# The inverse of a DeltaNet's 32x32 blocks, from 16x16 blocks and a merge on TensorE

## The chip, the cores and the metric

The kernel runs on one core of one Trainium2 chip. The metric is the device time of one execution in microseconds. The core has five engines that work side by side: PE (TensorE, matmuls; PEld is its weight load), DVE (VectorE), ACT (ScalarE), POOL (GpSimd) and SP, which issues DMAs. Each serves its own queue in order and waits on semaphores for the others.

## What is computed

One layer of a hybrid network over 640 tokens (128 context, 512 latent) with 1024 channels: a combined input projection, a bidirectional gated DeltaNet beside a short gated convolution, a gated merge, and a SwiGLU feed-forward network. The part that matters here is the DeltaNet's chunk step. For each direction, head and chunk of 64 tokens it inverts a unit lower triangular 64x64 matrix:

```python
kb = k * beta[..., None]
lower = jnp.where(tri_strict, jnp.einsum('bhncd,bhned->bhnce', kb, k) * decay, 0.0)
eye = jnp.eye(CHUNK, dtype=jnp.float32)
tmat = lax.linalg.triangular_solve(eye + lower, jnp.broadcast_to(eye, lower.shape),
                                   left_side=True, lower=True)
u = jnp.einsum('bhnce,bhned->bhncd', tmat, v * beta[..., None])
```

There are 2 directions x 8 heads x 10 chunks = 160 such matrices, and the inverse `tmat` feeds the sequential scan over the chunks.

## The kernel before

All large products are done as three single-pass matmuls of split operands (`mm3`, lines 83 to 85): the weights arrive by DMA, ACT casts a high part `wh` (line 57) and DVE subtracts to get a low part `wl` (line 58). One projection tile of 128 channels is 2 x 8 x 3 = 48 matmuls of 320 columns that write the PSUM tile `d`. These projections are independent of the DeltaNet's chain, and PE runs them between the DeltaNet's small matmuls.

The DeltaNet is done for two heads at a time, in four pairs. `run` calls `prep(p)` and `scan(p)` for each pair with projections (`zgate`, `gate_th`, `short`) between. The calls carry priorities (1000 for `prepare`, 300000 for `scan`), and a list scheduler sorts all instructions of the program into one fixed order per engine by priority, readiness and its own idea of durations. On the chip each engine then keeps to its order, and waits where an operand is late.

`prepare` goes through these steps for one pair. It transposes q, k, v to token layout, normalises them (`ss`, `rn` and the short chain of lines 71 to 77), makes `kh`, `kt` and `bv`, transposes `kh` and `qh` on PE (line 479) and forms the decay matrices `em` and `ea`. Line 528 forms the products and lines 532 to 534 multiply them in. Then comes the inverse:

- `Md` receives the 32x32 diagonal blocks of `em`, one block per row of 32 partitions, 20 of them (2 directions x 2 heads x 5), for four quadrants of partitions (`quad`). A 32x32 block transposition on DVE (line 550) turns this into `B`, in which every partition holds one whole 32x32 block.
- Lines 551 and 552 set `X` to -B with ones on the diagonal. The loop in lines 553 to 558 is a forward substitution, all 128 partitions at once: for j = 1 to 30 a product of column j of B with row j of X (line 556, into `otmp`) and a subtraction from the rows below (line 558). These are 60 DVE instructions per pair, each needing the one before, with (31 - j) j elements per partition, 30 to 240.
- Lines 562 and 563 transpose back to `RT` (transposed inverses) and `R`, and ACT copies them into `EW` (lines 565, 566).
- The merge of two 32x32 inverses into the 64x64 inverse is done on PE: 40 matmuls of 32x32 (line 575) into PSUM tile `v`, an ACT copy `Y` (line 580), 40 more (lines 586, 587), which go in turn to four places of the array, and scaled copies into `EW` (lines 590, 592).

`scan` (line 611 on) takes `EW`: products with `kt` (line 611), then eight sequential steps of small matmuls (line 640), copies to `RS` by ACT and DVE (lines 644, 658), the output products (line 670), a normalisation on DVE (`so`, `ro`, `ob`, lines 675 to 680) and a transposition of `ob` on PE (line 684).

POOL makes `KU` (line 459), `qh`, `kl` and the triangular masks, and issues DMAs. The PSUM pools for `v`, `s` and `w` have one buffer each.

Of the kernel before, what the change touches and what calls it, by code (L numbers as in the profile page):

```python
# [9 lines left out]
F32 = mybir.dt.float32  # L10
# [3 lines left out]
ALU = mybir.AluOpType  # L14
# [4 lines left out]
P = 128  # L19
# [18 lines left out]
class Kernel:  # L38
# [369 lines left out]
    def prepare(self, p, qkv):  # L408
        nc, dn, dc, g = self.nc, self.da, self.dc, self.g
        mm = nc.tensor.matmul  # L410
# [6 lines left out]
        for j in (1, 0, 2):  # L417
            pw = self.psw.tile([P, 1024], F32, name="w", tag="w")
            for t in range(NT):
                nc.tensor.transpose(pw[:, t * P:(t + 1) * P], qkv[j][:, t * P:(t + 1) * P], self.ident)  # L420
            x = dn.tile([P, TOK], F32, name="tk", tag="t25")
            (nc.scalar.copy, nc.scalar.copy, nc.scalar.copy)[j](out=x, in_=pw[:, 0:TOK])
            tok[j] = x
        q, k, v = (tok[j] for j in range(3))
# [31 lines left out]
        for c2 in range(2):  # L456
            s = half(1 - c2)
            for d in range(2):
                nc.gpsimd.tensor_tensor(out=KU[s, d, c2], in1=bc(g["egl"][s, d, :, h2], 64),
                                        in0=self.ident[s, s].unsqueeze(1).unsqueeze(1).broadcast_to([64, NT, 2, 64]),  # L460
                                        op=ALU.mult)
# [14 lines left out]
        for j, x in enumerate((kh, qh)):  # L476
            pw = self.psw.tile([P, 1024], F32, name="w", tag="w")
# [17 lines left out]
        for c2 in range(2):  # L495
            for t_, d, i in ((em, 0, 0), (em, 1, 2), (ea, 0, 0), (ea, 1, 1)):
                nc.sync.dma_start(out=t_[c2 * 64:c2 * 64 + 64, d].rearrange("p h t x -> p (h t x)"),
                                  in_=g["scr"][i, c2, h2].rearrange("h t x -> (h t x)").unsqueeze(0).broadcast_to([64, TOK]))
# [7 lines left out]
        for c2 in range(2):  # L506
            s = slice(c2 * 64, c2 * 64 + 64)
            o = em[s].rearrange("p d h t x -> p (d h t) x")
            nc.gpsimd.affine_select(out=o, in_=o, pattern=[[0, 20], [-1, 64]], compare_op=ALU.is_gt, fill=NEG,
                                    base=0, channel_multiplier=1)  # L510
            o = fm(ea[s, 0])
            nc.gpsimd.affine_select(out=o, in_=o, pattern=[[0, 10], [1, 64]], compare_op=ALU.is_ge, fill=NEG,
                                    base=0, channel_multiplier=-1)
            o = fm(ea[s, 1])
# [7 lines left out]
        for hd in range(2):  # L522
            hs = slice(hd * 64, hd * 64 + 64)
            pw = self.psw.tile([P, 1024], F32, name="w", tag="w")
            for t in range(NT):
                for c2 in range(2):
                    n = 2 * t + c2
                    mm(pw[c2 * 64:c2 * 64 + 64, t * P:(t + 1) * P], lhsT=kq3[hs, 0, n, :], rhs=kq3[hs, :, n, :],
                       start=True, stop=True)
# [5 lines left out]
        for c2 in range(2):  # L535
            nc.gpsimd.dma_start(out=AQ[half(c2), :, c2].rearrange("p d h t x -> p d (h t x)"),
                              in_=ea[half(c2)].rearrange("p d h t x -> p d (h t x)"))


        Md, EW = self.Md, self.EW  # L540
        emv = em.rearrange("p d h t x -> p (d h t) x")
        Ev = [EW[:, :, c2].rearrange("p d h t x -> p d (h t) x") for c2 in range(2)]
        quad = [(c2, b, slice(c2 * 64 + b * 32, c2 * 64 + b * 32 + 32)) for c2 in range(2) for b in range(2)]
        for c2, b, s in quad:
            cp = (nc.vector.tensor_copy, nc.scalar.copy)[b]
            cp(out=Md[s, 0:20], in_=emv[s, :, b * 32:b * 32 + 32])
        B = dn.tile([P, 32, 32], F32, name="blk", tag="kb")
        X = dn.tile([P, 32, 32], F32, name="X")
        tmp = dn.tile([P, 256], F32, name="otmp")
        nc.vector.transpose(out=B.rearrange("q r x -> q x r"), in_=Md.rearrange("p m x -> p x m"))  # L550
        nc.vector.tensor_scalar(out=X, in0=B, scalar1=-1.0, scalar2=None, op0=ALU.mult)
        nc.vector.memset(X.rearrange("q r x -> q (r x)")[:, 0:32 * 32:33], 1.0)
        for j in range(1, 31):
            n = 31 - j
            t = tmp[:, 0:n * j].rearrange("q (a b) -> q a b", b=j)
            nc.vector.tensor_tensor(out=t, in0=B[:, j + 1:32, j:j + 1].broadcast_to([P, n, j]),  # L556
                                    in1=X[:, j:j + 1, 0:j].broadcast_to([P, n, j]), op=ALU.mult)
            nc.vector.tensor_tensor(out=X[:, j + 1:32, 0:j], in0=X[:, j + 1:32, 0:j], in1=t, op=ALU.subtract)  # L558

        RT = dn.tile([P, 32, 32], F32, name="RT", tag="kb")  # L560
        R = dn.tile([P, 32, 32], F32, name="R")
        nc.vector.transpose(out=RT.rearrange("p m x -> p x m"), in_=X)
        nc.vector.transpose(out=R.rearrange("p m x -> p x m"), in_=X.rearrange("q r x -> q x r"))
        for c2, b, s in quad:
            nc.scalar.copy(out=Ev[c2][s, 0, :, b * 32:b * 32 + 32], in_=RT[s, 0:10])
            nc.scalar.copy(out=Ev[c2][s, 1, :, b * 32:b * 32 + 32], in_=R[s, 10:20])
# [2 lines left out]
        pw = self.psv.tile([P, 1024], F32, name="v", tag="v")  # L569
        Y = dn.tile([P, 20, 32], F32, name="Y")  # L570
        for m in range(20):
            for c2 in range(2):
# [3 lines left out]
                   tile_position=(c2 * 64 + 32, c2 * 64))  # L576
# [159 lines left out]
    def run(self):  # L736
# [121 lines left out]
        dast, da = stack("da")  # L858
# [15 lines left out]
        nc.gpsimd.memset(self.EW, 0.0)  # L874
        self.Md = da.tile([P, 32, 32], F32, name="Md")
        nc.gpsimd.memset(self.Md, 0.0)
        pre = {}

        def prep(p):
# [549 lines left out]
```

## Time and profile before

| | us |
|---|---|
| median of 3 runs | 1088.66 |
| lowest, highest | 1086.5, 1089.34 |
| the profiled execution | 1085.4 |
| its span in the profile | 1083.6 |
| PE busy | 1024.1 |
| DVE busy | 835.8 |

The span runs from the first to the last instruction of the profile; the execution's own time adds 1.8 us around it. Busy times are the union of an engine's instructions. PE's matmuls overlap, so a busy PE is not a PE at its peak. DeltaNet work lies between about 85 and 460 us. [...]

### The profile page before, as it was taken

The page shows a single profiled execution, that of the slowest core. Times are in us where ns is not written, and L with a number is a line of the kernel's source. Part 1 is how long each engine was busy: PE and PEld are TensorE (multiplying, and loading weights), DVE is VectorE, ACT ScalarE, POOL GpSimd, SP SyncE. Part 2 cuts the span into 40 slices and gives each one's busy share as a digit, 9 for nine tenths or more (in the row PEclk, how much of TensorE's full clock was granted, in tenths as well). Part 3 has the DMA queues.
Part 4 walks back from the last instruction along what each step waited for, and adds up shares of the span by engine and source line. Part 5 has one row for each costly group of instructions (what it writes and reads, how often), then busy time and mean ns, then how long its engine had stood idle before and what let it go on. Part 6 is the DMA issues. An engine that isn't in the chain of part 4 may idle for free.

```text
span 1083.6 us, 19702 instructions
## 1 busy us (share of the span) xinstructions
PE 1024.1 (95%) x7729; PEld 929.0 (86%) x7729; DVE 835.8 (77%) x1698; ACT 484.4 (45%) x929; POOL 138.9 (13%) x168
## 2 busy tenths in 40 slices
PE   6999978988988989999998998999999999999997
PEld 3699978887887888899996887999999999788885
DVE  5767896997898897995995789888777775975336
ACT  5568436417524324434223466444445444623321
POOL 2215321062062150101000000000000000000000
PEclk9999989998998999999998998999999999999999
DMA  9435712264164276547953532323222222552214
GB/s 343 147 91 135 206 52 67 72 152 113 42 164 125 68 171 202 182 151 246 318 167 116 185 108 89 103 85 98 94 79 78 98 81 76 177 173 96 81 39 156
DMA packets 47399, 141.52 MB, mean 131 GB/s; under 512 B 9517, under 2 KB 10034, under 8 KB 47306
## 3 DMA queue, kind: packets, MB, share of 16 engines
q1 hardware_dynamic: 42746, 127.10, 36.1%
q0 software_dynamic: 4560, 13.15, 5.4%
q8 instruction: 61, 1.00, 0.4%
q14 instruction: 32, 0.26, 0.1%
HBM read 117.57 MB, written 12.18 MB: 120 GB/s over the span
## 4 chain that ended last, share of the span: by engine, by line
PE 69%; DVE 14%; DMA 2%; ACT 2%; issue 2%; SPq 0%; DVEq 0%; POOL 0%; ACTq 0%
PE acc L1163 21%; PE d L84 7%; PE d L85 7%; PE d L83 7%; PE acc L84 6%; PE acc L83 6%; PE acc L85 6%; PE d L1163 3%; DVE X L558 3%; PE s L640 2%; DVE otmp L556 2%; DVE wl L58 1%; PE v L611 1%; PE v L670 1%; DMA ea<-scr 1%
## 5 line engine op out<-in xcount | busy, mean ns | idle before, releaser
L83 PE MATMUL d<-hT,wh 128*128 128x320 f32 x720 | 227.8, 317 | 1.2 <-DVE cy L721 1.1
L84 PE MATMUL d<-hT,wh 128*128 128x320 f32 x720 | 228.6, 318 | 0.0
L85 PE MATMUL d<-hT,wl 128*128 128x320 f32 x720 | 227.8, 317 | 0.4 <-DVE wl L58 0.4
L57 ACT CAST wh<-wr 128x512 fp32r<-128x512 f32 x150 | 87.8, 618 | 143.2 <-PE d L84 74.4
L83 PEld LDWEIGHTS d<-hT,wh 128*128 128x128 f32 x720 | 137.3, 191 | 3.9 <-DVE cy L721 1.7
L85 PEld LDWEIGHTS d<-hT,wl 128*128 128x128 f32 x720 | 137.3, 191 | 3.2 <-issue 0.7
L84 PEld LDWEIGHTS d<-hT,wh 128*128 128x128 f32 x720 | 137.1, 191 | 2.9 <-issue 0.3
L58 DVE TENSOR_TENSOR wl<-wr,wh 128x512 fp32r<-128x512 f32 x150 | 104.2, 717 | 36.4 <-ACT wh L57 35.2
L1163 PE MATMUL acc<-mh,wl 128*128 128x320 f32 x280 | 86.9, 310 | 1.8 <-DVE wl L1098 1.8
L83 PE MATMUL acc<-wh,as 128*128 128x512 f32 x220 | 85.7, 390 | 2.1 <-ACT as L1297 2.1
L1163 PE MATMUL acc<-mh,wh 128*128 128x320 f32 x280 | 87.0, 311 | 0.3 <-ACT early L1177 0.3
L196 DVE SCALAR_TENSOR_TENSOR gacc<-wr,cv,gacc 128x1024 f32<-128x1024 f32 x64 | 80.1, 1278 | 9.1 <-DMA wr<-in_w_mod_dram 7.2
L1163 PE MATMUL acc<-ml,wh 128*128 128x320 f32 x280 | 86.7, 310 | 0.0
L84 PE MATMUL acc<-wl,as 128*128 128x512 f32 x220 | 85.6, 389 | 0.0
L85 PE MATMUL acc<-wh,as 128*128 128x512 f32 x220 | 85.5, 389 | 0.0
L1102 ACT CAST wh<-wr 128x512 fp32r<-128x512 f32 x66 | 40.6, 622 | 72.0 <-PE acc L1163 37.0
L1102 ACT CAST wh<-S 128x512 fp32r<-128x512 f32 x88 | 54.1, 619 | 36.4 <-PE d L1163 19.6
L1098 DVE TENSOR_TENSOR wl<-S,wh 128x512 fp32r<-128x512 f32 x88 | 60.0, 686 | 3.9 <-ACT wh L1102 3.0
L1098 DVE TENSOR_TENSOR wl<-wr,wh 128x512 fp32r<-128x512 f32 x66 | 45.3, 689 | 19.1 <-ACT wh L1102 18.2
L1163 PEld LDWEIGHTS acc<-mh,wl 128*128 128x128 f32 x280 | 52.8, 188 | 2.1 <-DVE wl L1098 2.0
L1163 PEld LDWEIGHTS acc<-mh,wh 128*128 128x128 f32 x280 | 52.7, 188 | 0.6 <-ACT early L1177 0.6
L1163 PEld LDWEIGHTS acc<-ml,wh 128*128 128x128 f32 x280 | 52.8, 189 | 0.0
(365 smaller groups left out, 2348.9 us busy)
## 6 DMA issues: line engine op xcount, KB each, us to landing
wr<-in_w_ffn_in_dram SPq DMA_DIRECT2D x48, 512.0 KB, 3.7
wr<-in_w_in_dram SPq DMA_DIRECT2D x45, 512.0 KB, 3.5
wr<-in_w_mod_dram SPq DMA_DIRECT2D x32, 512.0 KB, 4.0
wr<-in_w_ffn_out_dram SPq DMA_DIRECT2D x22, 512.0 KB, 3.4
mr<-in_w_mod_dram SPq DMA_DIRECT2D x16, 512.0 KB, 8.5
thd<-gt SPq DMA_DIRECT2D x16, 320.0 KB, 4.1
bth<-thd SPq DMA_DIRECT2D x16, 320.0 KB, 3.0
wr<-in_w_br_dram SPq DMA_DIRECT2D x8, 512.0 KB, 6.9
```

Of the source, the lines that this page charges most:

```text
L57: (high or nc.scalar.copy)(out=hi[:, s], in_=raw[:, s])
L58: (low or nc.vector).tensor_tensor(out=lo[:, s], in0=raw[:, s], in1=hi[:, s].bitcast(F32), op=ALU.subtract)
L83: mm(out, lhsT=ah, rhs=bh, start=start, stop=False)
L84: mm(out, lhsT=ah, rhs=bl, start=False, stop=False)
L85: mm(out, lhsT=al, rhs=bh, start=False, stop=stop)
L196: nc.vector.scalar_tensor_tensor(out=acc[v], in0=w, scalar=self.cv[:, k, v:v + 1], in1=acc[v], op0=ALU.mult, op1=ALU.add)
L556: nc.vector.tensor_tensor(out=t, in0=B[:, j + 1:32, j:j + 1].broadcast_to([P, n, j]), in1=X[:, j:j + 1, 0:j].broadcast_to([P, n, j]), op=A ...
L558: nc.vector.tensor_tensor(out=X[:, j + 1:32, 0:j], in0=X[:, j + 1:32, 0:j], in1=t, op=ALU.subtract)
L640: mm(ps[half(c2), o:o + 64], lhsT=w(d, c2, t, hd), rhs=R[:, d, c2, t, hd, :], start=True, stop=True)
L1098: tt = lambda o, a, b, op: nc.vector.tensor_tensor(out=o, in0=a, in1=b, op=op)
L1102: nc.scalar.copy(out=dst[0], in_=src)
L1163: nc.tensor.matmul(ps, lhsT=A[x][:, k], rhs=B[y][:, k], start=start and k == 0 and n == 0, stop=k == 3 and n == 2, skip_group_check=True)
```

## The change

The 32x32 block in a partition is now treated as two 16x16 diagonal blocks and one 16x16 block below the diagonal. `two` is a view of both diagonal blocks at once. The forward substitution runs on them together: 14 steps in place of 30, 28 instructions in place of 60, with 2 (15 - j) j elements each. After the transpositions, PE makes the missing block for each of the 80 blocks: a first group of 80 matmuls of 32x16 (line 571), an ACT copy into `Y16` (line 573), a second group of 160 matmuls with 16 rows of weights (lines 579, 581; half of them for `RT`, half for `R`), and two DVE subtractions into `RT` and `R` (lines 583, 585). The merge to 64x64 follows as before (now from line 598). `X` and `Y16` become tiles that live through all pairs and are cleared once by POOL.

```diff
-        B = dn.tile([P, 32, 32], F32, name="blk", tag="kb")
-        X = dn.tile([P, 32, 32], F32, name="X")
-        tmp = dn.tile([P, 256], F32, name="otmp")
-        nc.vector.transpose(out=B.rearrange("q r x -> q x r"), in_=Md.rearrange("p m x -> p x m"))
-        nc.vector.tensor_scalar(out=X, in0=B, scalar1=-1.0, scalar2=None, op0=ALU.mult)
-        nc.vector.memset(X.rearrange("q r x -> q (r x)")[:, 0:32 * 32:33], 1.0)
-        for j in range(1, 31):
-            n = 31 - j
-            t = tmp[:, 0:n * j].rearrange("q (a b) -> q a b", b=j)
-            nc.vector.tensor_tensor(out=t, in0=B[:, j + 1:32, j:j + 1].broadcast_to([P, n, j]),
-                                    in1=X[:, j:j + 1, 0:j].broadcast_to([P, n, j]), op=ALU.mult)
-            nc.vector.tensor_tensor(out=X[:, j + 1:32, 0:j], in0=X[:, j + 1:32, 0:j], in1=t, op=ALU.subtract)
+        B = dn.tile([P, 33 * 32], F32, name="blk", tag="kb")
+        tmp = dn.tile([P, 128], F32, name="otmp")
+        sq32 = lambda a: a[:, 0:1024].rearrange("q (r x) -> q r x", x=32)
+
+        two = lambda a: a.rearrange("q (u w) -> q u w", u=2)[:, :, 0:512].rearrange("q u (a b) -> q u a b", b=32)[:, :, :, 0:16]
+        Bd, Xd = two(B), two(X)
+        nc.vector.transpose(out=sq32(B).rearrange("q r x -> q x r"), in_=Md.rearrange("p m x -> p x m"))
+        nc.vector.tensor_scalar(out=Xd, in0=Bd, scalar1=-1.0, scalar2=None, op0=ALU.mult)
+        nc.vector.memset(X[:, 0:32 * 32:33], 1.0)
+        for j in range(1, 15):
+            n = 15 - j
+            t = tmp[:, 0:2 * n * j].rearrange("q (u a b) -> q u a b", u=2, b=j)
+            nc.vector.tensor_tensor(out=t, in0=Bd[:, :, j + 1:16, j:j + 1].broadcast_to([P, 2, n, j]),
+                                    in1=Xd[:, :, j:j + 1, 0:j].broadcast_to([P, 2, n, j]), op=ALU.mult)
+            nc.vector.tensor_tensor(out=Xd[:, :, j + 1:16, 0:j], in0=Xd[:, :, j + 1:16, 0:j], in1=t, op=ALU.subtract)
...
+        pw = self.psv.tile([P, 1024], F32, name="v", tag="v")
+        for m in range(20):
+            for c2, b, s in quad:
+                mm(pw[s, m * 16:m * 16 + 16], lhsT=emv[s, m, b * 32:b * 32 + 32], rhs=RT[s, m, 16:32], start=True, stop=True,
+                   tile_position=(s.start, s.start))
+        nc.scalar.copy(out=Y16[:, :, 16:32], in_=pw[:, 0:320].rearrange("p (m x) -> p m x", x=16))
+        pw = self.psv.tile([P, 1024], F32, name="v", tag="v")
+        for m in range(20):
+            for c2, b, s in quad:
+                h = slice(s.start, s.start + 16)
+                o = m * 16
+                mm(pw[s, o:o + 16], lhsT=R[h, m], rhs=Y16[h, m, 16:32], start=True, stop=True,
+                   tile_position=(s.start, s.start))
+                mm(pw[s, 512 + o:512 + o + 16], lhsT=Y16[h, m], rhs=R[h, m, 0:16], start=True, stop=True,
+                   tile_position=(s.start, s.start))
+        nc.vector.tensor_tensor(out=RT[:, 0:20, 16:32], in0=RT[:, 0:20, 16:32],
+                                in1=pw[:, 0:320].rearrange("p (m x) -> p m x", x=16), op=ALU.subtract)
+        nc.vector.tensor_tensor(out=R[:, 0:20, 0:16], in0=R[:, 0:20, 0:16],
+                                in1=pw[:, 512:832].rearrange("p (m x) -> p m x", x=16), op=ALU.subtract)
...
+        self.X = da.tile([P, 33 * 32], F32, name="X")
+        nc.gpsimd.memset(self.X, 0.0)
+        self.Y16 = da.tile([P, 20, 32], F32, name="Y16")
+        nc.gpsimd.memset(self.Y16, 0.0)
```

The change also moves what stands around the inverse, since the scheduler sorts anew. On PE before, at the second pair, the first merge group (line 575, from `RT` and `em`) follows 83 projection matmuls after the transposition of the first scan's `ob`:

```order
L83 MATMUL d<-hT_75,wh 128x320
L84 MATMUL d<-hT_76,wh 128x320
L85 MATMUL d<-hT_75,wl 128x320
L83 MATMUL d<-hT_75,wh 128x320
L575 MATMUL v<-RT,em 32x32 x40
L84 MATMUL d<-hT_76,wh 128x320
```

On PE of the change, at the same place, the transpositions of `ob` and `kh` and the first new group (line 571) stand close together, and line 579 begins the second group:

```order
L707 MATMUL v<-ident,ob 128x128 x5
L85 MATMUL d<-hT_75,wl 128x320
L83 MATMUL d<-hT_75,wh 128x320
L84 MATMUL d<-hT_76,wh 128x320
L479 MATMUL w<-ident,kh 128x128 x5
L85 MATMUL d<-hT_75,wl 128x320
L83 MATMUL d<-hT_75,wh 128x320
L571 MATMUL v<-RT,em 32x16 x80
L84 MATMUL d<-hT_76,wh 128x320
L85 MATMUL d<-hT_75,wl 128x320
L83 MATMUL d<-hT_75,wh 128x320
L84 MATMUL d<-hT_76,wh 128x320
```

Five projection matmuls now stand between `ob` and the first group, and four between the first and the second; behind the second group eight precede line 598 (the former 575). From the first scan's last output matmuls to the first group it was 144 projection matmuls before and is 53 now.

On DVE of the change, at the second scan's end, between `so` (line 698, formerly 675) and `ob` (line 703, formerly 680), the end of the third pair's substitution and both transpositions stand; these ten rows are a part of that piece:

```order
L561 TENSOR_TENSOR X<-X,otmp 128x2x2x13
L75 TENSOR_TENSOR ont<-ro 128x10
L559 TENSOR_TENSOR otmp<-blk,X 128x28
L76 TENSOR_TENSOR ont<-ont,onxh 128x10
L561 TENSOR_TENSOR X<-X,otmp 128x2x14
L77 SCALAR_TENSOR_TENSOR ro<-ont,ro 128x10
L565 STREAM_TRANSPOSE RT<-X 128x32x32
L75 TENSOR_TENSOR ont<-ro 128x10
L58 TENSOR_TENSOR wl<-wr,wh 128x512
L76 TENSOR_TENSOR ont<-ont,onxh 128x10
```

Before, ten larger instructions of the substitution and `kh` stood between `so` and `ob` there, and the transpositions came later.

## Rows read from the trace of the kernel before

**Rows 1.** Page, busy time by engine: us (share of the span) xinstructions.

```profile
PE 1024.1 (95%) x7729; PEld 929.0 (86%) x7729; DVE 835.8 (77%) x1698; ACT 484.4 (45%) x929; POOL 138.9 (13%) x168
```

**Rows 2.** Windows by stage: window, us, busy us (xinstructions) by engine, granted clock, DMA share, GB/s.

```profile
118.00:165.00 47.00, 41.07 (x268) 40.54 (x267) 44.66 (x114) 19.76 (x32) 10.92 (x10) 0.93 0.38 114
165.00:247.00 82.00, 74.28 (x872) 66.57 (x870) 70.67 (x166) 34.51 (x68) 21.59 (x25) 1.00 0.39 99
247.00:331.00 84.00, 76.05 (x856) 68.98 (x856) 72.21 (x172) 40.73 (x74) 26.06 (x30) 0.94 0.41 106
331.00:420.00 89.00, 81.49 (x1101) 73.46 (x1102) 74.17 (x156) 36.86 (x74) 25.06 (x29) 0.96 0.46 129
```

**Rows 3.** Windows, a stretch in which PE runs projections alone.

```profile
149.00:165.00 16.00, 16.00 (x111) 16.00 (x110) 15.10 (x45) 7.33 (x12) 0.00 (x0) 1.00 0.23 75
```

**Rows 4.** Chain that ended last, 85 to 450 us, shares by line.

```profile
by line: PE d L84 10.2%; PE d L85 9.6%; PE d L83 9.4%; DVE X L558 7.6%; PE s L640 6.7%; DVE otmp L556 6.3%; DVE wl L58 4.2%; issue 3.0%; PE v L611 2.9%; DMA ea<-scr 2.3%; DVE RT L562 2.2%; PE v L670 2.0%; DMA AQ<-ea 1.8%; PE w L528 1.7%; PE
```

**Rows 5.** Waits of PE, 85 to 490 us: waiter, releaser, total us, times, longest.

```profile
PE v L575 <- DVE RT L562: 9.6, 4, 4.5
PE w L479 <- DVE kh L448: 7.4, 3, 5.9
PE v L670 <- DVE RS L644: 5.3, 3, 2.6
PE v L684 <- DVE ob L680: 2.0, 1, 2.0
PE v L586 <- ACT Y L580: 1.7, 2, 0.9
...
```

**Rows 6.** Windows of the granted clock's four low stretches (first, last, sum).

```profile
141.10:147.90 6.80, 5.36 (x21) 5.39 (x22) 6.67 (x10) 0.00 (x0) 3.79 (x3) 0.50 0.18 60
...
332.30:339.10 6.80, 5.73 (x118) 5.37 (x122) 6.73 (x8) 4.99 (x10) 3.46 (x3) 0.50 0.37 98
sum 23.80, PE 20.91 PEld 20.07 DVE 20.05 ACT 10.76 POOL 12.39; mean PE 5.23 PEld 5.02 DVE 5.01 ACT 2.69 POOL 3.10
```

**Rows 7.** Windows of line 556 alone, then of line 558 alone.

```profile
85.00:450.00 365.00, 42.56 (x120) 0.97 0.46 125
...
85.00:450.00 365.00, 50.93 (x120) 0.97 0.46 125
```

**Rows 8.** Groups by form, 85 to 450 us: busy us, mean ns of one, idle before.

```profile
L556 DVE TENSOR_TENSOR otmp<-blk,X 128x30 f32<-128x30 f32 x8 | 1.4, 177 | 0.2
L556 DVE TENSOR_TENSOR otmp<-blk,X 128x108 f32<-128x108 f32 x8 | 2.2, 270 | 0.2
L558 DVE TENSOR_TENSOR X<-X,otmp 128x220 f32<-128x220 f32 x8 | 7.9, 982 | 0.1
L556 DVE TENSOR_TENSOR otmp<-blk,X 128x240 f32<-128x240 f32 x8 | 3.2, 401 | 0.0
L562 DVE STREAM_TRANSPOSE RT<-X 128x1024 f32<-128x1024 f32 x4 | 7.8, 1959 | 0.1
L563 DVE STREAM_TRANSPOSE R<-X 128x1024 f32<-128x1024 f32 x4 | 8.2, 2053 | 0.0
L592 DVE TENSOR_SCALAR EW<-v 32x320 f32<-32x320 f32 x8 | 3.9, 490 | 0.8 <-ACT EW L590 0.5
```

**Rows 9.** Timeline of PE, first merge group of the third and fourth pairs.

```profile
333.37 2.46 PE L575 MATMUL v<-RT,em 32*32 32x32 f32 x80 [4.48 <-DVE RT L562]
...
403.99 1.55 PE L575 MATMUL v<-RT,em 32*32 32x32 f32 x80 [0.99 <-DVE RT L562]
```

**Rows 10.** Timeline of PE, fourth pair, second merge group's end.

```profile
410.41 0.19 PE L586 MATMUL v<-Y,R 32*32 32x32 f32 x2
...
410.70 0.19 PE L587 MATMUL v<-R,Y 32*32 32x32 f32 x1
410.82 0.41 PE L84 MATMUL d<-hT,wh 128*128 128x320 f32 x1
411.07 0.31 PE L85 MATMUL d<-hT,wl 128*128 128x320 f32 x1
```

More of the change, by code (lines that the diff above doesn't have):

```diff
@@ L537, in prepare @@
                               in_=ea[half(c2)].rearrange("p d h t x -> p d (h t x)"))
-        Md, EW = self.Md, self.EW
+        Md, EW, X, Y16 = self.Md, self.EW, self.X, self.Y16
         emv = em.rearrange("p d h t x -> p (d h t) x")
@@ L561, in prepare @@
         R = dn.tile([P, 32, 32], F32, name="R")
-        nc.vector.transpose(out=RT.rearrange("p m x -> p x m"), in_=X)
-        nc.vector.transpose(out=R.rearrange("p m x -> p x m"), in_=X.rearrange("q r x -> q x r"))
+        nc.vector.transpose(out=RT.rearrange("p m x -> p x m"), in_=sq32(X))
+        nc.vector.transpose(out=R.rearrange("p m x -> p x m"), in_=sq32(X).rearrange("q r x -> q x r"))
+        pw = self.psv.tile([P, 1024], F32, name="v", tag="v")
[3 more added lines that the diff above has]
+                   tile_position=(s.start, s.start))
```

## The prediction

> **What bounds the kernel now.** I read the engines' busy time first: PE is busy 95% of the span and VectorE 77% [rows 1], so PE is the bound on average, and the question is what this one stage pays. The DeltaNet stage runs from 118 to 420 us, and the windows [rows 2] cut it at the moments when RT is ready. In its four windows PE is idle 47 - 41.1 + 82 - 74.3 + 84 - 76.1 + 89 - 81.5 = 29.1 us, while VectorE is busy 86 to 95%. The chain of waits says the same from the other side: lines 558 and 556, the forward substitution, hold 7.6 + 6.3% of 365 us, or 51 us [rows 4]. So in this stage VectorE is nearly as full as PE, and its X chain is what PE waits behind.
>
> Which waits: PE waited 9.6 us for RT, 7.4 for kh, 5.3 for RS, 2.0 for ob and 1.7 for Y [rows 5]. Idle time has a second price. [...] At half speed 23.8 us do the work of 11.9. So the most that PE can win back here is 29.1 + 11.9 = 41.0 us. After 420 us PE has its projections left and I take that part as it is.
>
> **The change, part by part.**
>
> *Removed from VectorE.* The 240 instructions of lines 556 and 558 took 42.56 + 50.93 = 93.5 us [rows 7]. The new chain has 28 per pair, 112 in all, with 28 to 112 elements each. From the rows for 30 elements (177 ns) and 108 (270 ns) [rows 8], which give 1.19 ns per element, the 28 sum to 6.6 us, so 26.5 us over four pairs. Two subtractions from PSUM per pair come in; the nearest row, a 320-element read from PSUM, takes 490 ns [rows 8], so 3.9 us. VectorE loses about 63 us of work, some 15 us of which is stretching, by my estimate from forms like this one: line 558 took 982 ns with 220 elements where line 556 needed 401 for 240 [rows 8]. The smaller scaling and the wider memset at the head of the chain move under 1 us. X and Y16 are cleared once on GpSimd and Y16 is filled four times by ScalarE; they are busy 13% and 45% of the span [rows 1], so that I cost both at nothing but for the wait for the copy, below.
>
> *Added to PE.* 20 x 4 small matmuls in the first group and 20 x 8 in the second are 240 per pair. The trace shows two records for each fp32 matmul (80 records for 40 matmuls, [rows 9]), so 480 records per pair and 1920 in all. With four places of the array in turn, as here, 34 records of the old merge started within 0.29 us: 8.8 ns apart [rows 10]. 1920 x 8.8 ns = 16.9 us. Going back to projections costs too: from the last small record to the second projection passed 0.37 us where one step takes 16.00/111 = 0.144 [rows 3, 10], so about 0.2 us for each of 8 new groups, 1.6 us. Sum **+18.5 us**, and nothing covers it, since PE serves its queue in order and has other work ready. Bounds: half the record price if 16 columns in place of 32 halve it, 8.4 + 1.6 = 10 us; or 19 ns as for the group that has two places only (80 in 1.55 us, [rows 9]), 37 + 1.6 = 39 us, because the second group sends two matmuls to one place in a row. I take 8.8, as its row has the same four places.
>
> [...]
>
> *Taken off PE's waits.* The X chain is some 17 us shorter per pair ((93.5 - 26.5) / 4), four times the longest wait for RT, 4.5 us [rows 5]. I count the waits for RT as gone, -9.6 us, and with them the two low-clock stretches that lay at the long ones (6.8 us each, as in [rows 6]), which is 6.8 us of work. **-16.4 us.**
>
> *New waits.* Y16 is copied by ScalarE between the two groups, and the order gives PE 4 projections meanwhile, 0.58 us; the old wait for Y reached 0.9 us with more cover [rows 5]. The subtractions, 2 x 0.49 us, stand between the second group and line 598 with 8 projections, 1.15 us, as cover. I take 0.5 us for each of the 8 places, **+4 us** (0 to 7).
>
> *What is late next.* The shorter chain lets the scheduler close up the stage: counted in the order, the projections between the first scan's last matmuls and the second pair's first group shrink from 144 to 53. So kh, RS and ob are met with less cover. For the second scan's ob the order before had ten X instructions and kh between so and ob; now it has eight small ones and both transposes, 1.96 + 2.05 us [rows 8], which is about 1 us more under as many projections (54 and 55). The stretching of VectorE does not vanish with the X chain, it falls on whatever is there. I take 2 us for ob and 3 us of the 15 us of stretching, **+5 us**. Waits for kh and RS with their low clock I leave as they are.
>
> **Sum:** 18.5 - 16.4 + 4 + 5 = +11 us. Against the profiled execution, 1085.4 us (span 1083.6), this is 1096.5. That execution lies 3.3 us under the median of the runs, 1088.66, and 1.1 under the fastest; I add half the distance: **1098 us**.
>
> **Rivals.**
>
> A. *VectorE was the bound, and PE closes up.* For it: the 51 us of the X chain on the path [rows 4]. The deciding point is whether idle time and low clock fall from 41.0 below 41.0 - 18.5 = 22.5 us. If all waits for RT, kh, ob and Y went (20.7 us, [rows 5]), with the low clock but for the one short stretch of 3.4 us after RS (10.2 us), and the 4 us of new waits came, the sum is 18.5 + 4 - 30.9 = -8.4 us: 1077 on the profiled execution, some 1079 for the median. Against it: the kh wait of 5.9 us comes early in the stage, and the order still has most of the first pair's X chain ahead of kh.
>
> B. *The small matmuls run one by one.* At the 19 ns of [rows 9] the term is 39 us and the time 1098 + 20 = 1118; slower by much. For it: two in a row per place. It decides from about 13 ns per record upward, 8 us above my price. [...]
>
> C. *Both sides cancel.* Idle and low clock fall to between 19 and 26 us: no change, near 1089.
>
> D. *The chain is not shorter.* If views of two blocks with rows of 1 to 14 elements cost as much as 490 ns each [rows 8], the 112 take 55 us and RT is late again: 18.5 + 4 us with no gain, about 1111.
>
> **How the numbers follow.** The measurement can tell 0.3%, 3.3 us, from no change: faster is under 1085.4, slower over 1091.9. My forecast (its own range 1088 to 1107) gets 0.50, of which 0.06 falls within 0.3%; A 0.22, of which 0.02; B 0.13; C 0.12, all within; D 0.03. The forecast's 0.50 has another 0.04 on the faster side, for a record price at its low bound. Faster: 0.20 of A and these 0.04, 0.24. Same: 0.06 + 0.02 + 0.12 = 0.20. Slower: 0.40 + 0.13 + 0.03 = 0.56. The range takes in the low bound of the record price and most of A, and of B the lower part: 1080 to 1115.
>
> **What would show it.** In the changed profile: lines 559 and 561 should sum to 25 to 30 us; the new groups on lines 571, 579 and 581 should start 8 to 10 ns apart and take 4 to 5 us per pair; PE's wait for RT should be under 3 us; waits for Y16 and for the subtracted RT should show with 0.3 to 0.8 us each; waits for kh, ob and RS should remain. The scans should end earlier, with more projections left behind the fourth. If PE's idle time between 118 us and the last scan, with half of the low-clock time, is under 22 us, A is right and I am wrong; if the records stand over 12 ns apart, B.

## The result, and the profile after

The changed kernel takes **1137.51 us** (median of 4 runs, 1134.43 to 1141.61) against 1088.51 for the kernel before (4 runs, 1086.5 to 1089.34): ratio 1.0455, 95% interval 1.0413 to 1.0498. The forecast was 1098, with a range up to 1115. The profiled execution took 1135.12 us, its span is 1133.3 us, 49.7 more than before, and the mean granted clock, the share of PE's full speed that the profile shows as granted, is 0.957, where it was 0.979 before.

The page of the changed kernel, busy time by engine and the queue that brings instructions (packets, MB, share), with the queue's row of the kernel before behind it:

```profile
PE 1058.7 (93%) x9649; PEld 961.8 (85%) x9649; DVE 787.4 (69%) x1578; ACT 480.3 (42%) x929; POOL 145.1 (13%) x170
...
q8 instruction: 76, 1.25, 0.5%
```

```profile
q8 instruction: 61, 1.00, 0.4%
```

VectorE lost 48.4 us of busy time and PE gained 34.6 [rows 1]. Waits of PE in the changed kernel, 85 to 600 us (waiter, releaser, total us, times, longest):

```profile
PE v L581 <- issue: 13.2, 6, 4.8
PE v L579 <- issue: 6.4, 4, 2.6
PE w L479 <- DVE kh L448: 5.8, 2, 4.5
PE v L693 <- DVE RS L667: 3.8, 2, 2.2
PE v L707 <- DVE ob L703: 2.6, 2, 2.4
...
PE v L571 <- DVE RT L565: 2.0, 1, 2.0
...
PE v L571 <- issue: 1.7, 1, 1.7
```

The wait for RT went from 9.6 to 2.0 us, as forecast [rows 5]. New at the top stand 13.2 + 6.4 + 1.7 = 21.3 us of idle time inside the new groups that end with "issue": by the profile no operand, no semaphore and no buffer was late. The timeline of PE shows them at the second pair (start us, us, line, tile, shapes, count, and the idle time before):

```profile
228.01 1.53 PE L571 MATMUL v<-RT,em 32*32 32x16 f32 x160
...
230.47 0.21 PE L581 MATMUL v<-R,Y 16*32 16x16 f32 x3
235.44 0.18 PE L581 MATMUL v<-R,Y 16*32 16x16 f32 x1 [4.76 <-issue]
...
238.90 0.18 PE L581 MATMUL v<-R,Y 16*32 16x16 f32 x1 [1.51 <-issue]
...
242.35 0.18 PE L581 MATMUL v<-R,Y 16*32 16x16 f32 x1 [1.51 <-issue]
```

The first group ran its 160 records in 1.53 us. The second stopped at 230.68, ran from 235.44 to 237.38, stopped, and so on, with 3.46 and 3.45 us from one restart to the next. In the trace the packets of the instruction queue start at 236.53, 240.00 and 243.46, the same 3.46 us apart. How many instructions one holds follows from the page: 1920 records and as many weight loads came in [rows 1], 3840 instructions, and 15 packets, so 256 per packet, 128 records.

The clock fell too. Its five long low stretches in the changed kernel (window, us, busy us by engine, granted clock, DMA share, GB/s):

```profile
145.80:166.30 20.50, 15.82 (x461) 14.66 (x450) 2.72 (x5) 7.29 (x15) 0.00 (x0) 0.50 0.22 75
214.10:220.90 6.80, 6.12 (x57) 6.01 (x58) 6.70 (x14) 1.44 (x2) 3.44 (x8) 0.50 0.54 106
234.50:251.60 17.10, 13.14 (x399) 12.54 (x399) 2.27 (x4) 6.56 (x14) 0.00 (x0) 0.50 0.21 53
319.90:333.50 13.60, 10.36 (x238) 9.82 (x239) 3.14 (x6) 6.17 (x13) 0.00 (x0) 0.50 0.09 32
412.00:429.10 17.10, 14.72 (x428) 13.81 (x427) 2.40 (x3) 5.46 (x12) 0.96 (x1) 0.50 0.48 160
```

Four of them lie on the four second groups. In the first pair the clock had fallen at 145.8, ahead of that group: PE had waited 2.04 us for RT, up to 144.6. Before the change no low stretch of the stage was longer than 6.8 us [rows 6]; this one is 20.5. With two more of 3.4 us it is 81.9 us between 85 and 520, of which PE was busy 66.6; before it was 23.8 with 20.9 busy [rows 6]. And PE's busy time in the same 435 us, before and then after:

```profile
85.00:520.00 435.00, 404.21 (x4140) 372.47 (x4139) 371.86 (x778) 192.69 (x358) 111.43 (x126) 0.97 0.48 137
```

```profile
85.00:520.00 435.00, 390.50 (x5704) 356.16 (x5704) 298.88 (x625) 175.11 (x333) 115.90 (x126) 0.91 0.41 114
```

So idle time rose from 30.8 to 44.5 us. A budget of the 49.7 us: the 1920 records at the 8.5 ns that line 571 shows at the full clock, 16.3; idle time, +13.7; busy time at the low clock, 66.6 - 20.9 = 45.7 us more, half of it lost, +22.9. Together 52.9, 3 us over; behind 520 us, which the budget leaves out, the low clock is 6 us shorter than before (14.7 us against 20.9). By this count the largest part is the clock, the next the records, then the idle time. What each would be worth without the others it doesn't show.

### The profile page after: what moved, and what is told of

It reads as the page before. It is cut to its first block, busy times and chain, and to the rows that moved or that the text cites. A ratio compares the mean times of both kernels' runs of the same rounds, so it can differ in the third digit from the quotient of the medians.

```text
span 1133.3 us, 23436 instructions
## 1 busy us (share of the span) xinstructions
PE 1058.7 (93%) x9649; PEld 961.8 (85%) x9649; DVE 787.4 (69%) x1578; ACT 480.3 (42%) x929; POOL 145.1 (13%) x170
## 3 DMA queue, kind: packets, MB, share of 16 engines
q8 instruction: 76, 1.25, 0.5%
## 4 chain that ended last, share of the span: by engine, by line
PE 68%; DVE 12%; issue 4%; DMA 2%; ACT 2%; POOL 1%; SPq 0%; DVEq 0%; POOLq 0%; ACTq 0%
PE acc L1190 20%; PE d L84 8%; PE d L83 8%; PE d L85 7%; PE acc L84 5%; PE acc L85 5%; PE acc L83 5%; PE d L1190 3%; PE s L663 2%; DVE otmp L559 1%; DVE X L561 1%; PE v L581 1%; PE v L693 1%; PE v L598 1%; PE w L528 1%
## 5 line engine op out<-in xcount | busy, mean ns | idle before, releaser
L85 PE MATMUL d<-hT,wl 128*128 128x320 f32 x720 | 233.3, 325 | 0.4 <-DVE wl L58 0.4
L84 PE MATMUL d<-hT,wh 128*128 128x320 f32 x720 | 232.2, 323 | 0.0
L83 PE MATMUL d<-hT,wh 128*128 128x320 f32 x720 | 231.7, 323 | 0.0
L85 PEld LDWEIGHTS d<-hT,wl 128*128 128x128 f32 x720 | 140.8, 196 | 4.0 <-issue 0.7
L84 PEld LDWEIGHTS d<-hT,wh 128*128 128x128 f32 x720 | 140.8, 196 | 2.3 <-issue 0.5
L83 PEld LDWEIGHTS d<-hT,wh 128*128 128x128 f32 x720 | 140.7, 196 | 1.9 <-issue 0.2
L1125 DVE TENSOR_TENSOR wl<-wr,wh 128x512 fp32r<-128x512 f32 x66 | 45.3, 689 | 19.5 <-ACT wh L1129 18.5
```

Of the source, the lines that this page charges most:

```text
L83: mm(out, lhsT=ah, rhs=bh, start=start, stop=False)
L84: mm(out, lhsT=ah, rhs=bl, start=False, stop=False)
L85: mm(out, lhsT=al, rhs=bh, start=False, stop=stop)
L1125: tt = lambda o, a, b, op: nc.vector.tensor_tensor(out=o, in0=a, in1=b, op=op)
```

## The experiments

Theory 1 says that the dense small matmuls outrun the supply of PE's instructions, and that the pauses bring the clock down. Theory 2 says that small matmuls hold the clock down by themselves. Theory 3, that matmuls in one place or buffer stop each other. "Issue" and "low" below are PE's idle time ended by nothing and the time at 0.50, both from 85 to 520 us; the changed kernel has 21.3 and 81.9.

**The two parts alone.** First the substitution without lines 568 to 586, which are both groups, the copy and the subtractions:

```diff
         nc.vector.transpose(out=R.rearrange("p m x -> p x m"), in_=sq32(X).rearrange("q r x -> q x r"))
-        pw = self.psv.tile([P, 1024], F32, name="v", tag="v")
-        for m in range(20):
...
-        nc.vector.tensor_tensor(out=R[:, 0:20, 0:16], in0=R[:, 0:20, 0:16],
-                                in1=pw[:, 512:832].rearrange("p (m x) -> p m x", x=16), op=ALU.subtract)
```

> This kernel has the two 16x16 forward substitutions on VectorE and none of the new small matmuls, subtractions or the copy to Y16; the quarter of each 32x32 inverse that the merge would fill keeps what the tile held, so its output is not the reference's. The PE stream is then the one of before. By the steps of the prediction the waits for RT go (-16.4 us) and later waits grow (+5 us): about 1077 us, against 1088.5 before. If VectorE's 63 us of work had been covered by PE's other work, 1086 to 1090. Theory 1 (the new groups outrun the supply of PE's instructions): no idle time of over 0.5 us ended by nothing (issue) on PE in the stage, and low-clock time of 30 us or less.

Measured 1083.6 us, ratio 0.9966 (0.9941 to 0.9991): 4.5 us faster than before, where 11 were expected. Its largest waits:

```profile
PE w L479 <- DVE otmp L559: 4.5, 1, 4.5
PE v L688 <- ACT sq L430: 3.9, 1, 3.9
PE v L579 <- issue: 3.6, 2, 3.0
PE w L479 <- DVE kh L448: 3.3, 2, 2.1
PE v L674 <- DVE RS L648: 2.5, 2, 2.4
PE v L579 <- DVE RT L565: 2.0, 1, 2.0
```

RT's wait fell by 7.6 us. Waits at line 479, whose operand is still `kh` behind a VectorE queue, were 7.4 and are 7.8, and `sq` and two pauses of the old merge (here line 579) came in. Idle time fell by 4.4 us only, and the low clock did not fall: 27.3 us. The chain did get shorter: the last transposition of `ob` starts at 422.0 us, where it was 462.1 before (485.7 in the changed kernel). But PE is as busy as before, 1023.6 us against 1024.1, so that 40 us less of chain were worth 4.5 us.

Then both groups and the copy to `Y16` on the old substitution, with nobody to read the results:

```diff
         nc.vector.transpose(out=R.rearrange("p m x -> p x m"), in_=X.rearrange("q r x -> q x r"))
+        pw = self.psv.tile([P, 1024], F32, name="v", tag="v")
+        for m in range(20):
+            for c2, b, s in quad:
+                mm(pw[s, m * 16:m * 16 + 16], lhsT=emv[s, m, b * 32:b * 32 + 32], rhs=RT[s, m, 16:32], start=True, stop=True,
+                   tile_position=(s.start, s.start))
...
```

> The kernel before with its 32x32 substitution, plus the 240 small matmuls per pair and the copy to Y16; nobody reads their results. This isolates what the small matmuls cost PE. At the price of the prediction (8.8 ns per record, 8 switches) it would be 1088.5 + 18.5 = 1107 us. Theory 1 (instruction supply): the second group of each pair stops after each 128 records as in the changed kernel, 4 to 8 us of such idle time per pair, and the clock falls there: 1088.5 + 18.5 + 14 to 20 of pauses + 10 to 20 of low clock = 1125 to 1145 us. If the pauses come from the shorter VectorE chain or the subtractions, no pauses and 1107 us.

Measured 1142.67 us, 1.0501 (1.0463 to 1.0538): 54.6 us over its own kernel before (1088.11). Issue 18.1, low 95.6. From the substitution alone to the changed kernel it is 53.9. The groups cost the same 54 us on either substitution, so that the cost is theirs and needs neither VectorE's shorter chain nor the subtractions.

**The order inside the second group.**

```diff
                 mm(pw[s, o:o + 16], lhsT=R[h, m], rhs=Y16[h, m, 16:32], start=True, stop=True,
                    tile_position=(s.start, s.start))
+            for c2, b, s in quad:
+                h = slice(s.start, s.start + 16)
+                o = m * 16
                 mm(pw[s, 512 + o:512 + o + 16], lhsT=Y16[h, m], rhs=R[h, m, 0:16], start=True, stop=True,
```

> The changed kernel with the second group in another order: for each m the four matmuls of the first kind at the four places in turn, then the four of the second kind, so that no two in a row go to one place; same instructions. Theory 3 (two in a row at one place, or writing one PSUM bank pair, stop the array): the pauses go and the time falls by 15 to 30 us, to 1108 to 1122. Theories 1 and 2: the pauses stay at 18 to 24 us, the time stays within 5 us of 1137.5.

1140.43 us, 1.0505 (1.0441 to 1.0568), issue 22.5, low 88.7. Nothing changed; theory 3 falls in this form.

**Wider matmuls.**

```diff
-                mm(pw[s, o:o + 16], lhsT=R[h, m], rhs=Y16[h, m, 16:32], start=True, stop=True,
+                mm(pw[s, o:o + 64], lhsT=R[h, m], rhs=Yf[h, m * 32 + 16:m * 32 + 80], start=True, stop=True,
```

(and line 581 likewise).

> The changed kernel with 64 columns in place of 16 in each of the 160 matmuls of the second group: the same number of instructions, four times the columns; the 48 extra columns land where the next matmul of the same place writes, so nothing else changes. Theory 1 (instruction supply: 128 records per packet, one packet in about 3.5 us): the columns run in what was idle, the pauses of the second group shrink from 21 us to under 6, the group takes as long as before to within 1 us per pair, and the low clock in the stage falls from 82 us to under 45; time 1115 to 1138. Theory 2 (the clock falls because small matmuls leave most of the array unused, with or without pauses): pauses shrink but the low clock stays near 80 us, and the time is 1135 to 1150. If PE was limited by its own work in the group, 1280 records at 64 columns add 15 to 25 us: 1150 to 1165.

1146.35 us, 1.0524 (1.0486 to 1.0563): 8.8 us over the changed kernel, for four times the columns. Issue fell to 14.7 and low did not (92.2). That is a miss for theory 1's time and speaks for theory 2: in the first pair the group ran from 149.19 to 158.6 with one pause of 0.35 us, and the clock was 0.50 throughout. But it had fallen at 146.9, behind PE's wait of 1.86 us for RT and before this group's first record at 147.53.

**Fewer of them, and the first group alone.** The first edit puts `if m < 10 or b:` and `if m >= 10 or not b:` before the two matmuls of the second group and puts 4 matmuls of 160 columns ahead of them, which fill the places left out; the other deletes the second group and the subtractions.

> The changed kernel without the 40 matmuls per pair of the second group whose result nobody reads; 4 matmuls of 160 columns fill their place in PSUM, so that the subtractions stay as they are. It sizes the marginal price of a small matmul: at 8.8 ns per record 320 records less are 3 us, 1134 to 1137 us. Theory 1 (27 ns per record, 3.46 us per 128): 8.6 us less, and one pause less per pair, 1127 to 1132. Theory 2 with half speed (13 ns): 1131 to 1135.

1138.36 us, 1.043 (1.040 to 1.046): the same as the changed kernel, although three packets fewer were fetched (73). Issue is 16.5, low 92.2; one pause of 5.9 us moved into the first group. A quarter less of the second group bought nothing that can be told: the two intervals leave room for the 3 us that 320 records cost at 8.8 ns as well as for nothing, and theory 1's 8.6 us and one pause less per pair did not show.

> The changed kernel with the first group (80 small matmuls per pair) and the copy to Y16, without the second group and the subtractions; the inverse stays unmerged, so its output is not the reference's. From 1083.6 us without any group: at a third of the groups' 54 us, 1101 to 1103. Theory 1 (instruction supply): 320 instructions pass one or two packet ends, so at most one pause of 2 us per pair: records 5.6 us, pauses 2 to 7, low clock under 45 us: 1091 to 1099. If the clock falls at the first group already for as long as now (70 us or more of low clock): 1100 and over.

1101.18 us, 1.0101 (1.0066 to 1.0137), 17.6 over the substitution alone, a third of 54. The kernel before took 1090.52 us beside this run and 1088.11 beside the other; set against those, it is 15.2. Issue 5.8, low 34.1 as expected; the time is 2 us over theory 1's range, no more than the two times of the kernel before differ. Its profile has five packets more than the substitution alone (65 against 60) for 640 records and 640 weight loads: 256 each again.

**In pieces.** Each piece of a few rows `m` gets its own tile of the one PSUM buffer, and the copy or subtractions follow it at once, with a higher priority for the scheduler (`urgent`); the second group of the 14 pieces:

```diff
-        pw = self.psv.tile([P, 1024], F32, name="v", tag="v")
-        for m in range(20):
...
+        for m0 in range(0, 20, 2):
+            pw = self.psv.tile([P, 1024], F32, name="v", tag="v")
+            for m in range(m0, m0 + 2):
...
+            with self.urgent():
```

> The changed kernel with the same 240 small matmuls per pair cut into 14 pieces (4 of 20, then 10 of 16), each with its own PSUM tile of the one buffer, so that PE has to let the copy or the subtractions of a piece end before the next and runs 3 to 8 projections between. VectorE and ScalarE get more, smaller instructions. Theory 1 (instruction supply): a packet of 256 instructions now holds over 3 us of work, so idle time ended by nothing falls from 21 us to under 5 in the stage and low-clock time from 82 us to under 45; with 14 switches per pair at 0.2 us (11 us) and the 16.9 us of records the time is 1100 to 1115. Theory 2 (the small matmuls hold the clock down, pauses or not, and a short rest of projections does not bring it back): low clock stays over 60 us, 1120 to 1140. Theory 3 (the turn-around of the one PSUM buffer becomes the wait): idle time ended by ACT or DVE at the pieces of 0.3 us or more each, 17 us and up, 1125 to 1145.

> As the kernel with 14 pieces, but the second group in 5 pieces of 32 matmuls (5 to 8 projections between): half the rest per matmul. Theory 1: 138 PE instructions in about 1.3 us is still faster than one packet of 256 in about 3.5 us, so pauses remain, 5 to 12 us together, with low clock of 40 to 60 us; time between the 14 pieces and the changed kernel, 1110 to 1128. Theory 3 (turn-around): fewer turn-arounds, so faster than the 14 pieces.

1158.7 us (1.0626, 1.0578 to 1.0673) for 14 pieces and 1148.33 (1.0528, 1.0508 to 1.0548) for 9. Both went the wrong way. Issue fell to 8.7 and 6.2, but low rose to 126.3 and 95.6 us, where theory 1 had it fall. Theory 3's waits for the buffer did not come: no wait of PE for a piece's copy or subtraction stands in the list of its waits for the 14 pieces. The first low stretch of the 14:

```profile
139.70:177.20 37.50, 35.06 (x637) 29.41 (x637) 14.16 (x35) 9.94 (x22) 2.89 (x3) 0.50 0.15 47
```

PE was busy 35 of these 37.5 us, with small matmuls and projections in turn, and the clock stayed down. Neither theory alone could explain that, so the next two kernels measured the clock apart from the DeltaNet.

**Stretches behind the end of the kernel.** To the kernel before, stretches of PE work are added behind the last output, each between 100 projections (`rest`). Of this kernel and of the next there is one execution each:

```diff
+        rest(100)
+        small(240)
+        rest(100)
+        small(240, hb)
+        rest(100)
+        small(240, w=64)
+        rest(100)
+        for _ in range(14):
+            small(16)
+            rest(4)
...
```

> The kernel before, with a row of stretches behind its last output that measure the disputed costs by themselves on PE, each between 100 projections of 320 columns (128x128): (a) 240 small matmuls at four places while 12 MB are loaded, (b) the same in bfloat16, one weight load and one record each, (c) with 64 columns, (d) 14 times 16 small ones and 4 projections, (e) 60 full 128x128 matmuls with 16 columns, (f) 28 times 8 small ones and 8 projections, (g) as (a) with no other transfers. Theory 1 (instruction supply): (a) and (g) stop every 128 records, 3.5 us from packet to packet in (a) and less in (g) if the transfers share the DMA engines; (b) holds 480 instructions in place of 960 and stops half as often; (c) stops less; (d), (e) and (f) do not stop. If the clock follows the pauses alone, it falls in (a), (b), (g) only and is 1.0 in (d) and (f). Theory 2 (small matmuls hold the clock down): it falls in (a) to (d), in (d) for most of its 12 us, and comes back in the projections that follow.

Timeline of (a), (b)'s end, (c) and (g), and the windows of (c), (d), (e), (f):

```profile
1104.73 2.29 PE L1393 MATMUL ps<-raw 32*32 32x16 f32 x252
1109.13 1.75 PE L1393 MATMUL ps<-raw 32*32 32x16 f32 x128 [2.10 <-issue]
1113.17 1.16 PE L1393 MATMUL ps<-raw 32*32 32x16 f32 x70 [2.28 <-issue]
...
1136.70 0.34 PE L1393 MATMUL ps<-hb 32*32 32x16 bf16 x26 [3.25 <-issue]
...
1153.27 3.87 PE L1393 MATMUL ps<-raw 32*32 32x64 f32 x258
1158.30 1.99 PE L1393 MATMUL ps<-raw 32*32 32x64 f32 x128 [1.16 <-issue]
1161.77 1.53 PE L1393 MATMUL ps<-raw 32*32 32x64 f32 x94 [1.48 <-issue]
...
1307.99 2.34 PE L1393 MATMUL ps<-raw 32*32 32x16 f32 x258
1312.71 1.26 PE L1393 MATMUL ps<-raw 32*32 32x16 f32 x128 [2.38 <-issue]
1316.46 1.47 PE L1393 MATMUL ps<-raw 32*32 32x16 f32 x94 [2.49 <-issue]
```

```profile
1153.30:1163.30 10.00, 7.36 (x482) 6.95 (x481) 0.00 (x0) 0.00 (x0) 0.00 (x0) 1.00 0.02 5
1178.10:1193.40 15.30, 15.30 (x502) 12.48 (x501) 0.00 (x0) 0.00 (x0) 0.00 (x0) 1.00 0.02 4
1208.80:1231.40 22.60, 22.60 (x122) 22.60 (x120) 0.00 (x0) 0.00 (x0) 0.00 (x0) 0.57 0.00 1
1248.20:1291.90 43.70, 43.70 (x665) 37.73 (x664) 0.00 (x0) 0.00 (x0) 0.00 (x0) 1.00 0.01 2
```

Exactly 128 records stand between two stops, with VectorE, ScalarE and GpSimd idle. (g) took 9.9 us for what 480 records at 8.5 ns do in 4.1. Four times the columns, (c), took 10.0: in the pauses they were nearly free. The bfloat16 stretch (b), with half the instructions (240 records where the others have 480, and as many weight loads), stopped once (3.25 us) and took 5.4 us. From restart to restart it took 4.04 us in (a), with other transfers running (DMA share 0.71), and 3.75 in (g) and 3.47 in (c), without them (0.02): traffic is not the cause of the pauses. This settles them as theory 1 has them; why the distance is not always the same stays open. The clock fell in (a) after the first pause, in (b) at the end of its one and in (g) in the second (means 0.75, 0.98 and 0.82), not in (c), whose pauses were 1.16 and 1.48 us, and not in (d) and (f). So small matmuls mixed with projections did not bring it down from 1.0 here, and theory 2 as stated falls. It also fell in (e), where the 120 full 128x128 records with 16 columns followed each other 188 ns apart without a pause: neither idle time nor a small array is the whole rule.

> The kernel before with other stretches behind its last output, again between 100 projections: (a) 240 small matmuls in a row, then at once 14 times 16 small ones and 4 projections; (b) 8 times 60 small ones and 24 projections; (c) 28 times 16 small ones and 4 projections from the full clock; (d) 240 small ones in a row; (e) 4 times a wait of PE for VectorE of 2 to 2.5 us and 8 projections. If the pauses alone bring the clock down, it falls in (a), (d) and (e) and not in (b) and (c). If it takes the small matmuls, it does not fall in (e). If a low clock stays low as long as small matmuls are mixed in, the 14 rounds of (a) run at 0.5 and those of (c) at 1.0. Price by theory 1 in (b): 8 to 10 ns per record and 0.3 us per round, no pauses, 5 to 5.5 us per round of 60 and 24; in (c) 1.15 us per round as measured before.

The windows of 13 of (a)'s 14 rounds and of (c)'s 28, then of (e):

```profile
1116.20:1142.00 25.80, 25.71 (x472) 21.15 (x472) 0.00 (x0) 0.00 (x0) 0.00 (x0) 0.50 0.01 3
...
1210.70:1242.30 31.60, 31.60 (x1006) 25.61 (x1005) 0.00 (x0) 0.00 (x0) 0.00 (x0) 1.00 0.01 4
...
1286.30:1299.60 13.30, 6.93 (x26) 5.87 (x27) 5.78 (x8) 0.00 (x0) 0.00 (x0) 0.67 0.00 0
```

The same round of 16 small matmuls and 4 projections takes 1.15 us when it starts at the full clock and stays there, and 1.92 us when it starts low, and it stays low too, at 0.50 for these 13 rounds, until projections alone follow (1.00 from 1157.3 on, in (b)). In (e) the clock fell at 1290.8, in the second of two waits of 1.65 and 1.57 us with 8 projections between: waits do it without any small matmul. That fits the 14 pieces: each of the four low stretches with pieces in them began within 2.2 us of the end of a wait or pause (4.46, 3.80, 1.25 and 2.60 us); three lasted until the pieces were through, the fourth ended two pieces before the last. It fits the first pair of the wider matmuls and of the changed kernel too. (b), 60 small ones and 24 projections, ran at 1.0 with no pause, 4.84 us per round: 120 records 8.5 ns apart and some 0.3 us for going to and fro.

**On the whole kernel.** Six pieces per pair (two of 10 rows `m`, then four of 5), and `hold` behind the copy or the subtractions of each keeps the next one off by small copies on ScalarE (copies, subtractions and `hold` are `urgent` again):

```diff
+        def hold(a):
+            nc.scalar.copy(out=jk[:, 0:1], in_=a)
+            for _ in range(8):
+                nc.scalar.activation(out=jl, in_=X[:, 0:256], func=AF.Copy, scale=jk[:, 0:1])
+            nc.scalar.activation(out=jk[:, 1:2], in_=a, func=AF.Copy, scale=jl[:, 0:1])
...
+                hold(pw[:, m0 * 16:m0 * 16 + 1])
```

> The changed kernel with the same 240 small matmuls per pair in 6 pieces (two of 40 in the first group, four of 40 in the second), and a chain of 10 small copies on ScalarE behind each piece that holds the one PSUM buffer for some 4 us, so that PE runs some 40 to 60 projections between two pieces. Nothing else is changed. Theory 1 (instruction supply): 160 instructions with 80 and more of the projections last 6 us or longer, so a packet of 256 is always there: issue pauses under 3 us in the stage, low clock at the level of before (20 to 40 us), and the price of the prediction is right: 1083.6 + 16.9 + 24 pieces at 0.3 us (7) + 0 to 6 = 1105 to 1114 us. Theory 2 (small matmuls hold the clock down however they are spread): low clock over 60 us and 1125 or more. Theory 3 (the longer chain of a pair, some 25 us more, comes onto the path): low clock and issue pauses as in theory 1, but over 15 us of new waits of PE for RT, Y or EW: 1115 to 1135.

1179.59 us (1.0828, 1.0809 to 1.0847). Up to 511 us it did what theory 1 says (0.2 us of issue, 23.9 us of low clock), but theory 3's long chain decided the time: the projections ran out before the last scan. The last 66 us before and 100 us behind that moment:

```profile
445.00:511.00 66.00, 61.92 (x881) 56.99 (x881) 32.29 (x84) 35.21 (x86) 15.27 (x21) 1.00 0.38 103
511.00:611.00 100.00, 39.09 (x587) 28.40 (x588) 62.94 (x84) 30.66 (x63) 10.42 (x13) 0.54 0.42 141
```

With 1 and 3 copies in the loop in place of 8:

> As the kernel with 6 pieces held apart by ScalarE, with 3 small copies in each hold in place of 10, so that the order gives PE 9 to 25 projections between two pieces, 1.3 to 3.7 us, and the chain of a pair grows by some 5 to 8 us against the changed kernel in place of 35. Theory 1 (instruction supply, and the clock that its pauses bring down): 160 instructions and 18 or more of the projections last 2.3 to 4.7 us, so issue pauses in the stage fall from 21 to under 8 us and low clock from 82 to under 50; 1083.6 + 16.9 of records + 24 pieces at 0.3 us (7) + 2 to 10 = 1110 to 1118 us, well under the changed kernel's 1137.5. If spreading does not help, or the longer chain costs as much as it saves, 1130 and over.

> As above with 5 small copies in each hold; the order gives PE 18 to 30 projections between two pieces, 2.6 to 4.4 us. Theory 1: issue pauses under 3 us and low clock under 40 us in the stage, the records and pieces at the same 24 us; the chain of a pair is some 12 us longer than with 3 copies, so that the fourth pair ends about 50 us later and the question is whether projections last: if they do, 1108 to 1115 us; if they run out ahead of the last scan, 1120 to 1145 with low clock behind 480 us.

1119.5 us (1.0278, 1.0253 to 1.0303) and 1121.47 (1.03, 1.0269 to 1.0332). The first is 18 us faster than the changed kernel with the same matmuls and more work on ScalarE; its largest waits of PE:

```profile
PE v L594 <- issue: 6.0, 4, 2.8
PE v L709 <- DVE RS L683: 4.6, 4, 3.1
PE w L479 <- DVE otmp L559: 4.5, 1, 4.5
```

Issue 9.2 and 2.7 us, low 41.0 and 31.9. Against the substitution alone the first has 37.6 us more span: 16.3 of records, 24 x 0.30 = 7.2 of switching, 6.7 of idle time, 4.5 for the low clock, together 34.7. The prices of a record and of a switch are those of the stretches, not measured apart in this kernel. So a third of the 54 us comes back by spreading, as theory 1 has it, and most of the rest is, by these prices, what the records and their switches cost. The first is 1.5 us over its range. The second is 6.5 us over its first range and inside the other, for projections that run out: they ended at 510.4 us, 8 us behind the last transposition of `ob`, PE then waited 7.2 us for ScalarE, and the clock was low from 515.4 to 525.6. Both are slower than the kernel before.

## Why the prediction was wrong

Its sign was right: the change costs PE more than VectorE's shorter chain gives back. Its size was not, 1098 against 1137.5. By its own steps:

- **Removed from VectorE**, 63 us: 48.4 on the page. Lines 559 and 561 took 18.8 + 18.0 = 36.8 us, not 26.5; their medians are 252 and 250 ns, but single ones reach 1.35 us.
- **Taken off PE's waits**, -16.4 us: mis-sized. The wait for RT went (9.6 to 2.0), but the low clock with it did not, and other waits took its place. The substitution alone gave 4.5 us, where this step and "what is late next" together had said 11. It began from VectorE "busy 86 to 95%" in the four windows of [rows 2]; the fourth says 74.17 of 89 us, 83%.
- **New waits**, +4 us: the waits for Y16 and for R (line 579) came to 0.4 and 0.6 us.
- **Added to PE**, +18.5 us: **the step that failed.** The price per record was right where instructions were there, 8.4 to 9.0 ns on line 571, four places in turn. What failed is its size: it held 1920 records and 8 switches and nothing else. PE had other work ready, as the step says, but not its instructions. The 8.8 ns came from 34 records in a row; the new groups are longer runs, and their records had to wait. They were to take 4 to 5 us per pair; at the second pair they ran from 228.01 to 243.2. This term and the new waits, 22.5 us together, measured 54 us, in two runs on two substitutions. The bound of 39 us came from one record after another; the price had no entry for instructions per us, and the clock was costed only at waits of before.
- **The clock.** "Waits for kh and RS with their low clock I leave as they are" left out that the new groups would make low stretches of their own: 81.9 us in place of 23.8.

Of the rivals B came nearest with its time, 1118, but not with its mechanism: two in a row at one place cost nothing that the other order saved. Its sign, records over 12 ns apart, showed only at the low clock: 13.7 ns from 235.44 on, but 9.4 ns over the 128 records from 317.62 on, at the full clock.

Rival A's point was idle time and half the low clock under 22 us. Between 85 and 520 us the changed kernel has 44.5 + 81.9 / 2 = 85 us, and the substitution alone did not reach it either: 26.4 + 27.3 / 2 = 40 us, where the same count gives 30.8 + 23.8 / 2 = 43 before (the 23.8 us at 0.50 of [rows 6]). VectorE was nearly full, 83 to 95% busy in the windows of [rows 2], but little waited for it that did not wait for something else next.

Open is what exactly the chip asks for before it gives the full clock back, and what leaving out the unneeded matmuls saves, which that run could not tell.

## What to carry to other kernels

Cost a run of small matmuls in instructions as well as in ns: here, while PE waited for them, 256 of its instructions came per 3.46 us at the second pair and per 3.47 to 4.04 us in the stretches, and an fp32 matmul had four (two weight loads and two records: 640 of each for the 320 of line 571), so that, behind the first stop, 64 small matmuls in a row took that long, with 16 columns as with 64. If they can't be fewer, spread them over long matmuls, so that 256 instructions hold more work than the 3.5 to 4 us in which the next ones came here, start them at the full clock (1.15 us a round against 1.92), and count 0.3 us for going to them and back, as in the rounds of 4.84 us. And before paying for a shorter chain on another engine, run the chain's shortening by itself: here it was worth 4.5 us.

## What the runs showed of the hardware

- Packets of PE's instructions held 256 (3840 more instructions, 15 more packets), and while PE waited for them they came 3.46 us apart at the second pair of the kernel and 3.47 to 4.04 us in the isolated stretches.
- The same mixture of small matmuls and projections kept whichever level of the clock it started with: 1.15 us a round at 1.00, 1.92 at 0.50.
- Records of 32x32 matmuls in four places started 8.5 ns apart with 16 columns (line 571, clock 1.00) and 8.8 with 32 [rows 10]; with 64, 14.2 in (c), at 1.00. Those of 128x128 ones with 16 columns started 188 ns apart, at a mean clock of 0.57.
